# A hybrid attention and RWKV7 block: q and k stored once per pair and loaded by heads, the first inverse step behind two other operations, and another order of four up products

## The chip, the cores and the metric

The kernel runs on one core of one Trainium2 chip. TensorE (PE) multiplies, VectorE (DVE), ScalarE (ACT) and GpSimd (POOL) work on tiles, and SyncE (SP) issues most of the DMA transfers; POOL issues some of them too. Each engine takes its own instructions in order. The metric is the device time of one launch in microseconds (us). A profiled execution shows what every engine and every DMA queue did.

## The reference

One block of width 1024 over a sequence of 1024: a norm and modulation, then two token mixers side by side on the same input, gated and summed, then a feed-forward part with a causal convolution of width 3.

```python
def token_mixer(u, w_in, ...):
    proj = u @ w_in
    p_fox, p_rwkv, p_gate = _split(proj, (FOX_COLS, RWKV_COLS, GATE_COLS))
    q, k, v, f = _split(p_fox, FOX_SPLITS)
    log_f = jax.nn.log_sigmoid((f + fox_b_f).astype(jnp.float32)).transpose(0, 2, 1)
    o_fox = fox_attention(to_heads(q), to_heads(k), to_heads(v), log_f)
    o_rwkv = rwkv7_time_mix(p_rwkv, ...)
    gate_fox, gate_rwkv = jnp.split(jax.nn.sigmoid(p_gate), N_BRANCHES, axis=-1)
    merged = gate_fox * (o_fox @ fox_w_out) + gate_rwkv * (o_rwkv @ rwkv_w_out)
    return merged @ w_o

def fox_attention(q, k, v, log_f):
    cum = jnp.cumsum(log_f, axis=-1)
    ...
        logits = jnp.einsum('bhqd,bhkd->bhqk', q[:, :, q0:q1], k[:, :, :q1]).astype(jnp.float32) * scale
        logits = logits + cum[:, :, q0:q1, None] - cum[:, :, None, :q1]
    ...

def rwkv7_time_mix(...):
    ...
    def step(state, inp):
        r_t, w_t, k_t, v_t, a_t, b_t = inp
        sa = jnp.einsum('bhvk,bhk->bhv', state, a_t)
        state = state * w_t[:, :, None, :] + sa[..., None] * b_t[:, :, None, :] + v_t[..., None] * k_t[:, :, None, :]
        y_t = jnp.einsum('bhvk,bhk->bhv', state, r_t)
        return state, y_t
    ...

def conv_ffn(u, w_up, conv_w, conv_b, w_down):
    a, b = jnp.split(u @ w_up, 2, axis=-1)
    a = lax.conv_general_dilated(a, conv_w[:, None, :], ..., feature_group_count=D_FF) + conv_b
    return (jax.nn.silu(a) * b) @ w_down
```

There are 8 attention heads and 8 RWKV heads of width 64, and the hidden width of the feed-forward part is 2816.

## The kernel before, in words

**Precision.** A 32-bit operand is split into a high and a low part, both in the reduced 32-bit form that PE multiplies fast. A product is three matmul groups: high by high, low by high, high by low. So a weight `in` becomes `hi_in` (a cast) and `lo_in` (a subtraction on DVE, L274), and a projection tile of 128x512 takes 3 x 8 matmuls (the input is `u_hi`, `u_lo`).

**Stages**, by the profile's time: the norm and modulation to 60 us; the input projections to 600, with the RWKV recurrence woven between them; a transition to 626, with the last gates and the first head loads; attention to 825, with the rest of the gate products (`rk_ps`) between its steps; the branch outputs to 910 and w_o to 1005; the up products to 1430; the down products to the end.

**What sets the order.** PE's order is the order in which the program is written out; a planner in the program (`Weave`) decides by added-up matmul costs when the next piece of the recurrence is put between projection tiles. In the projections, the instructions of DVE, ACT, POOL and SP are put in order by the framework's scheduler, which takes the dependences between tiles and its own estimates; DVE and ACT in attention, and all engines in the up part, are written by hand. A wait is for a tile: a tile name has a fixed number of buffers, and the next user of a buffer waits until the last reader of the old content is done, be it an engine or a DMA that stores it.

**q and k** (`qk_steps`, L385 ff.; i from 0 to 3 for q, 4 to 7 for k; one i is a pair of heads, two halves of the sequence each). ACT writes the high part `qh` from PSUM (L393), DVE the low part `ql` (L395), and SP stores both (L399) into `d_st`, a DRAM array of [8 heads, 4 blocks, 128 rows, 1024]: blocks 0 and 1 hold, in 64-row halves, q high over q low and k high over k high; blocks 2 and 3 hold q high and k low, with 4 rows of forget-gate sums below each (L664, L665). So one half is six stores of 64x512. `qh` and `ql` share the tile name `sp0`. PSUM banks for projections (`big`) are two.

**A unit of the recurrence** is a pair of heads and a half of the sequence: 8 units. `pre` (L697 ff.) loads the decay `cum` and `al` from `d_lora` (L711, L713), scans `cum` (L715), takes exponentials (`el`, `en` L721), builds `ar` and `bk`, makes E from the products p (L764), and sends its 32x32 blocks through DRAM (`sm`, L772, and `M`, L776) to invert unit triangular matrices: 31 steps of a product t (L784) and a sum into E (L786) on DVE, one after the other. The result goes back through DRAM (`se`) into TT. Then come transposes of v and ar (`vt`, `at`), the products `q` and their copy into QA (L823), and the head sums `bs`, from which `bon` is made (L827). `main` (L829 ff.) takes it up later: X (L842), `xi` on PE, `zi`, the state S and its products `sp` (L903).

**Gates.** In the projections a gate tile `gt` goes through ACT and DVE (L337 to L341) and is stored as `d_gate<-gs` (L342) from a tile that the next gate uses. From the transition on, gate products are made in one bank `rk_ps`, which ACT reads twice (`gs` L1162, `gm` L1163) before PE may write the next one.

**Heads.** `load_head` (L993 ff.) brings one head's q, k and v for attention with three POOL transfers: `stA` 128x2x1024 (1 MB), `stB` 68x2x1024 (544 KB) and `vh` (512 KB); each has two buffers. Attention multiplies from `stA` over 128 rows and from `stB` over 68.

**The up products** (`plan`, L1606; `up_product`, `up_evac`): the 22 x 128 columns of each half of the up weight are made in pairs by a seven-product scheme with operands `T1` to `T4` of the activations and sums of weights (S1, A22 and so on). An entry (i, k) of `plan` is one product k of pair i. An operand is cast by ACT (L1722 for T, L1481 for weights) and its low part subtracted on DVE (L1485), in the order in which the plan needs them.

## Time and profile before

| what | us |
|---|---|
| median of 3 runs | 1646.45 |
| lowest and highest | 1645.22, 1648.16 |
| the profiled execution's own time | 1648.91 |
| its span in the trace | 1647.1 |
| head loads: median from issue to landing of stA, stB, vh | 6.9, 13.9, 3.9 |
| a 128 KB store of qh or ql | 2.5 |
| a copy M<-sm | 2.7 |

The span is the time from the first to the last instruction in the trace; the run's time has 1.8 us more around it. A row of the timeline gives the start, the duration, the engine, the line, the operation with output<-inputs and, in brackets, how long the engine had been idle before and what ended that. Line 141 holds all matmuls, line 145 all transposes, so PE's rows are told apart by their tiles. SPq and POOLq rows are the issue of a transfer, not its flight. The granted clock is a share of TensorE's full clock.

### The profile page before, as it was taken

The page shows a single profiled execution, that of the slowest core. Times are in us where ns is not written, and L with a number is a line of the kernel's source. Part 1 is how long each engine was busy: PE and PEld are TensorE (multiplying, and loading weights), DVE is VectorE, ACT ScalarE, POOL GpSimd, SP SyncE. Part 2 cuts the span into 40 slices and gives each one's busy share as a digit, 9 for nine tenths or more (in the row PEclk, how much of TensorE's full clock was granted, in tenths as well). Part 3 has the DMA queues.
Part 4 walks back from the last instruction along what each step waited for, and adds up shares of the span by engine and source line. Part 5 has one row for each costly group of instructions (what it writes and reads, how often), then busy time and mean ns, then how long its engine had stood idle before and what let it go on. Part 6 is the DMA issues. An engine that isn't in the chain of part 4 may idle for free.

```text
span 1647.1 us, 25947 instructions
## 1 busy us (share of the span) xinstructions
PE 1607.8 (98%) x9694; PEld 1339.6 (81%) x9694; DVE 1222.6 (74%) x2373; ACT 820.9 (50%) x1537; POOL 130.8 (8%) x153
## 2 busy tenths in 40 slices
PE   7999999999999999999999999999999999999998
PEld 7777788798978788888888888788888888888886
DVE  5786787878876526888679447887777777886677
ACT  5563335445445646766623235644444444555455
POOL 0011101111111010221022000000000000000000
PEclk9999999999999999999999999999999999999999
DMA  8488645543332346433197420242232232675363
GB/s 339 138 326 242 178 123 143 134 123 94 107 115 85 97 126 157 129 117 106 56 353 270 168 81 26 84 134 97 96 119 98 96 109 96 225 254 160 122 211 109
DMA packets 121645, 240.59 MB, mean 146 GB/s; under 512 B 40048, under 2 KB 48880, under 8 KB 121520
## 3 DMA queue, kind: packets, MB, share of 16 engines
q1 hardware_dynamic: 113040, 220.58, 41.0%
q0 software_dynamic: 8480, 18.37, 4.2%
q8 instruction: 76, 1.25, 0.3%
q14 instruction: 49, 0.40, 0.1%
HBM read 173.35 MB, written 65.54 MB: 145 GB/s over the span
## 4 chain that ended last, share of the span: by engine, by line
PE 58%; DVE 5%; ACT 2%; DMA 2%; issue 1%; SPq 0%; ACTq 0%; DVEq 0%
PE X L141 13%; PE D L141 13%; PE Y L141 6%; PE wo L141 5%; PE br L141 4%; PE rk_ps L141 3%; PE W L141 3%; PE gt L141 3%; PE lg L141 2%; PE ov L141 2%; PE tp L145 2%; DMA d_gate<-gs 1%; DVE nm L1049 1%; DVE P L1059 1%; DVE tl L1089 0%
## 5 line engine op out<-in xcount | busy, mean ns | idle before, releaser
L141 PE MATMUL D<-op,op 128*128 128x512 f32 x924 | 209.8, 389 | 0.0
L141 PEld LDWEIGHTS D<-op,op 128*128 128x128 f32 x924 | 173.3, 188 | 36.3 <-DVE op L1261 0.3
L141 PE MATMUL X<-T_m,S 128*128 128x512 f32 x440 | 107.8, 390 | 1.6 <-ACT T_m L1722 1.1
L141 PEld LDWEIGHTS X<-T_m,S 128*128 128x128 f32 x440 | 82.4, 188 | 20.4 <-ACT T_m L1722 2.5
L1260 ACT CAST op<-g 128x512 fp32r<-128x512 f32 x77 | 47.8, 621 | 73.8 <-PE D L141 49.0
L1261 DVE TENSOR_TENSOR op<-g,op 128x512 fp32r<-128x512 f32 x77 | 53.0, 688 | 41.4 <-ACT op L1260 41.4
L1519 DVE SCALAR_TENSOR_TENSOR c<-ab,vec,c 128x512 f32<-128x512 f32 x88 | 65.9, 750 | 18.4 <-ACT c L1522 16.8
L784 DVE TENSOR_TENSOR t<-E,M 128x60 f32<-128x60 f32 (+24 forms) x248 | 55.6, 224 | 27.9 <-DMA M<-sm 21.8
L1485 DVE TENSOR_TENSOR A<-ur,A 128x512 fp32r<-128x512 f32 x64 | 44.0, 688 | 38.7 <-ACT A L1481 38.5
L1485 DVE TENSOR_TENSOR S<-ur,S 128x512 fp32r<-128x512 f32 x66 | 45.5, 691 | 35.2 <-ACT S L1481 35.1
L274 DVE TENSOR_TENSOR lo_in<-raw_in,hi_in 128x512 fp32r<-128x512 f32 x84 | 56.7, 712 | 17.6 <-PE gt L141 4.8
L1481 ACT CAST S<-ur 128x512 fp32r<-128x512 f32 x66 | 41.0, 622 | 55.8 <-DVE ur L1474 30.6
L141 PE MATMUL Y<-T_h,S 128*128 128x512 f32 x264 | 63.6, 390 | 0.4 <-ACT T_h L1740 0.4
L141 PE MATMUL Y<-T_h,A 128*128 128x512 f32 x264 | 63.7, 389 | 0.3 <-ACT T_h L1722 0.3
L1053 ACT ACTIVATE P<-lg,nm 128x896 f32<-128x896 f32 (+3 forms) x64 | 47.4, 743 | 30.7 <-DVE nm L1049 22.5
L1481 ACT CAST A<-ur 128x512 fp32r<-128x512 f32 x64 | 39.6, 622 | 43.1 <-PE X L141 31.3
L786 DVE TENSOR_TENSOR E<-E,t 128x60 f32<-128x60 f32 (+24 forms) x248 | 56.2, 227 | 6.4
L141 PE MATMUL W<-B_f,A 128*128 128x512 f32 x252 | 60.6, 389 | 0.0
L141 PE MATMUL X<-B_b,A 128*128 128x512 f32 x252 | 60.5, 389 | 0.0
L141 PEld LDWEIGHTS Y<-T_h,S 128*128 128x128 f32 x264 | 49.5, 188 | 11.1 <-ACT T_h L1740 0.8
L141 PEld LDWEIGHTS Y<-T_h,A 128*128 128x128 f32 x264 | 49.5, 188 | 10.9 <-ACT T_h L1722 0.7
L272 ACT CAST hi_in<-raw_in 128x1024 fp32r<-128x1024 f32 x42 | 43.8, 1048 | 26.3 <-PE ps_rkv L141 11.3
(483 smaller groups left out, 4134.4 us busy)
## 6 DMA issues: line engine op xcount, KB each, us to landing
raw_in<-in_w_in SPq DMA_DIRECT2D x50, 512.0 KB, 4.0
wm<-in_w_mod SPq DMA_DIRECT2D x48, 512.0 KB, 7.3
ur<-in_w_up SPq DMA_DIRECT2D x44, 512.0 KB, 3.8
g<-d_g SPq DMA_DIRECT2D x35, 512.0 KB, 4.0
d_g<-gs SPq DMA_DIRECT2D x44, 256.0 KB, 2.0
d_g<-c SPq DMA_DIRECT2D x33, 256.0 KB, 4.4
d_st<-qh SPq DMA_DIRECT2D x64, 128.0 KB, 2.5
stA<-d_st POOLq DMA_DIRECT2D x8, 1024.0 KB, 6.9
```

The costliest lines, as they stand in the source:

```text
L141: nc.tensor.matmul(o, lhsT, rhs, start=start, stop=stop, skip_group_check=more)
L145: nc.tensor.transpose(o, i, eye)
L272: nc.scalar.copy(hi, raw)
L274: nc.vector.tensor_tensor(lo[:, c : c + NH], raw[:, c : c + NH], f32(hi[:, c : c + NH]), op=ALU.subtract)
L784: tt(tv, E32[:, 0:J, s : s + 1].to_broadcast([128, J, W]), M32[:, s : s + 1, s + 1 : 32].to_broadcast([128, J, W]), op=ALU.mult)
L786: tt(E32[:, 0:J, s + 1 : 32], E32[:, 0:J, s + 1 : 32], tv, op=ALU.add)
L1053: nc.scalar.activation(e[:, 0:n], lg[:, 0:n], AF.Exp, bias=nm[:, 0:1], accum_out=nm[:, 1:2])
L1260: nc.scalar.copy(hi, src)
L1261: tt(lo, src, f32(hi), op=ALU.subtract)
L1481: nc.scalar.copy(hi, src)
L1485: tt(lo, src, f32(hi), op=ALU.subtract)
L1519: stt(c, ab[:, x + hf * NH : x + hf * NH + NH], V("conv_w", 22 * x + i), c, op0=ALU.mult, op1=ALU.add)
```

## The change

1. `d_st` is replaced by `d_qk` [4 pairs, 4 parts, 128 rows, 1024], with the parts q high, q low, k high, k low of both heads of a pair, and `d_f` for the forget-gate rows. One half of q or k is stored with two transfers of 128x512 (256 KB) in place of six of 64x512 (128 KB).
2. `load_head` picks a head's 64 rows out of `d_qk`: `stA` in two transfers of 64x2x1024, `stB` in one of 64x2x1024 and one of the 4 rows of `d_f`, and `vh` as before.
3. The first step of the first unit's inverse (the product t, L784) is ordered on DVE behind the copy QA<-q (L823) and behind `bon` (L827) of that unit.
4. In `plan` the products (1, 4) and (0, 5) change places, so that both products with T4 come ahead of both with T1.

```diff
--- before.py
+++ after.py
@@ -201,7 +201,8 @@
 
 
     d_gate = dr.tile([16, 128, S], F32, name="d_gate")
-    d_st = dr.tile([8, 4, 128, S], F32R, name="d_st")
+    d_qk = dr.tile([4, 4, 128, S], F32R, name="d_qk")
+    d_f = dr.tile([8, 2, 4, S], F32R, name="d_f")
     d_v = dr.tile([8, 128, 8, 128], F32R, name="d_v")
     d_orw = dr.tile([4, 128, S], F32, name="d_orw")
 
@@ -242,6 +243,12 @@
             nc.vector.tensor_tensor(dst[:, cs], ps, bb[:, cs], op=ALU.add)
 
     marks = {}
+    first_step = []
+
+    def after_this(i):
+        for x in first_step:
+            tc.add_manual_dep(x.ins, i.ins.name, NOSYNC)
+
     late_lo = deque()
 
     def lower(wait=0):
@@ -393,10 +400,8 @@
                 nc.scalar.activation(hi, ps, AF.Copy, scale=sc_)
                 lo = gsp.tile([128, NH], F32R, tag="sp0", name=f"ql{i}_{hf}")
                 stt(lo, ps, sc_, f32(hi), op0=ALU.mult, op1=ALU.subtract)
-                h0 = 2 * (i % 4)
-                for t, k, r0 in ((hi, 0, 0), (lo, 0, 64), (hi, 2, 0)) if i < 4 else ((hi, 1, 0), (hi, 1, 64), (lo, 3, 0)):
-                    for h in range(2):
-                        nc.sync.dma_start(f32(d_st[h0 + h, k, r0 : r0 + 64, cs]), f32(t[h * 64 : h * 64 + 64, :]))
+                for t, x in ((hi, 0), (lo, 1)) if i < 4 else ((hi, 2), (lo, 3)):
+                    nc.sync.dma_start(f32(d_qk[i % 4, x, :, cs]), f32(t))
 
         HS = (slice(0, 64), slice(64, 128))
 
@@ -661,8 +666,8 @@
                     nc.scalar.copy(r[:, 3, :], z)
                     nc.scalar.activation(r[:, 4, :], f32(r[:, 0, :]), AF.Copy, scale=-1.0)
                     nc.scalar.activation(r[:, 5, :], f32(r[:, 1, :]), AF.Copy, scale=-1.0)
-                    nc.sync.dma_start(f32(d_st[:, 2, 64:68, cs]), f32(r[:, 0:4, :]))
-                    nc.sync.dma_start(f32(d_st[:, 3, 64:68, cs]), f32(r[:, 2:6, :]))
+                    nc.sync.dma_start(f32(d_f[:, 0, :, cs]), f32(r[:, 0:4, :]))
+                    nc.sync.dma_start(f32(d_f[:, 1, :, cs]), f32(r[:, 2:6, :]))
 
             for p in range(4):
                 for i in (p, 4 + p):
@@ -781,8 +786,10 @@
             for s in range(31):
                 J, W = s // 4 + 1, 31 - s
                 tv = t32[:, 0 : J * W].rearrange("p (j w) -> p j w", w=W)
-                tt(tv, E32[:, 0:J, s : s + 1].to_broadcast([128, J, W]),
-                   M32[:, s : s + 1, s + 1 : 32].to_broadcast([128, J, W]), op=ALU.mult)
+                i = tt(tv, E32[:, 0:J, s : s + 1].to_broadcast([128, J, W]),
+                       M32[:, s : s + 1, s + 1 : 32].to_broadcast([128, J, W]), op=ALU.mult)
+                if k == 0 and s == 0:
+                    first_step.append(i)
                 tt(E32[:, 0:J, s + 1 : 32], E32[:, 0:J, s + 1 : 32], tv, op=ALU.add)
             se = scr.tile([2, NCU, 2, 32, 32], F32, tag="se", name=f"se{n}")
             for g in range(4):
@@ -820,11 +827,12 @@
             for c in range(NCU):
                 for h in range(2):
                     mm(q[HS[h], c * CH : c * CH + CH], E[HS[1 - h], c, h, 0, :], UV[HS[1 - h], c, h, :], start=True, stop=True)
-            nc.vector.tensor_copy(QA[:, :, 0, :], c3(q))
+            after_this(nc.vector.tensor_copy(QA[:, :, 0, :], c3(q)))
             bp = gen(f"bs{n}")
             yield from head_sums(bp, rkb, tmp("kr", dt=F32R), tmp("al", dt=F32R))
             bon = tmp("bon", bufs=2)
-            tt(bon, bp, vv, op=ALU.mult)
+            after_this(tt(bon, bp, vv, op=ALU.mult))
+            first_step.clear()
             units[p, hf] = dict(ready=ready, pcd=pcd, ar=ar, E=E, QA=QA, TT=TT, bon=bon, UV=UV)
 
         def main(k, p, hf):
@@ -991,10 +999,13 @@
     heads = {}
 
     def load_head(h):
+        rows = d_qk[h // 2, :, h % 2 * 64 : h % 2 * 64 + 64, :].rearrange("k r s -> r k s")
         A = at.tile([128, 2, S], F32R, tag="stA", name=f"stA{h}")
-        nc.gpsimd.dma_start(A, d_st[h, 0:2, :, :].rearrange("k r s -> r k s"))
+        nc.gpsimd.dma_start(A[0:64, :, :], rows[:, 0:3:2, :])
+        nc.gpsimd.dma_start(A[64:128, :, :], rows[:, 1:3, :])
         B = at.tile([128, 2, S], F32R, tag="stB", name=f"stB{h}")
-        nc.gpsimd.dma_start(B[0:68, :, :], d_st[h, 2:4, 0:68, :].rearrange("k r s -> r k s"))
+        nc.gpsimd.dma_start(B[0:64, :, :], rows[:, 0:4:3, :])
+        nc.gpsimd.dma_start(B[64:68, :, :], d_f[h].rearrange("k r s -> r k s"))
         vh = at.tile([128, 8, 128], F32R, tag="vh", name=f"vh{h}")
         i = nc.gpsimd.dma_start(vh, d_v[h])
         marks.setdefault("head", i)
@@ -1604,7 +1615,7 @@
         put(6, s1[:, NH:])
 
     plan = [(i, k) for ks in ((1, 2), (7,), (6,)) for i in range(2) for k in ks]
-    plan += [(0, 4), (0, 5), (1, 5), (1, 4), (0, 3), (1, 3)] + [(2, k) for k in (1, 7, 6, 2, 4, 5)]
+    plan += [(0, 4), (1, 4), (0, 5), (1, 5), (0, 3), (1, 3)] + [(2, k) for k in (1, 7, 6, 2, 4, 5)]
     for i in range(3, NFF):
         plan += [(i, 1), (i, 7), (i - 1, 3)] + [(i, k) for k in ((6, 2, 4, 5) if i < NFF - 1 else (6, 2, 5, 4))]
     plan.append((NFF - 1, 3))
```

**DVE, the first unit's inverse** (t and E are its steps; `ql_0`, `ql_1` low parts of q/k halves, `lo_in` a weight's low part). Before:

```order
L395 SCALAR_TENSOR_TENSOR ql_0_1605<-qk_0_1461,qh_0_1603 128x512
L784 TENSOR_TENSOR t_0_1504<-E_0_1502,M_0_1497 128x31
L786 TENSOR_TENSOR E_0_1502<-E_0_1502,t_0_1504 128x31
L823 COPY QA_0_1426<-q_0_1638 128x8x64
...
L784 TENSOR_TENSOR t_0_1504<-E_0_1502,M_0_1497 128x48
L827 TENSOR_TENSOR bon_0_1679<-bs_0_1656,v_639 128x512
L786 TENSOR_TENSOR E_0_1502<-E_0_1502,t_0_1504 128x2x24
L274 TENSOR_TENSOR lo_in_1716<-raw_in_1713,hi_in_1715 128x512
L784 TENSOR_TENSOR t_0_1504<-E_0_1502,M_0_1497 128x69
L274 TENSOR_TENSOR lo_in_1716<-raw_in_1713,hi_in_1715 128x512
L395 SCALAR_TENSOR_TENSOR ql_1_1705<-qk_1_1613,qh_1_1703 128x512
```

After (the line numbers are those of the changed kernel):

```order
L402 SCALAR_TENSOR_TENSOR ql_0_1582<-qk_0_1438,qh_0_1580 128x512
L830 COPY QA_0_1407<-q_0_1611 128x8x64
L834 TENSOR_TENSOR bon_0_1652<-bs_0_1629,v_640 128x512
L789 TENSOR_TENSOR t_0_1481<-E_0_1479,M_0_1474 128x31
L281 TENSOR_TENSOR lo_in_1685<-raw_in_1682,hi_in_1684 128x512
L793 TENSOR_TENSOR E_0_1479<-E_0_1479,t_0_1481 128x31
L281 TENSOR_TENSOR lo_in_1685<-raw_in_1682,hi_in_1684 128x512
L402 SCALAR_TENSOR_TENSOR ql_1_1678<-qk_1_1586,qh_1_1676 128x512
L789 TENSOR_TENSOR t_0_1481<-E_0_1479,M_0_1474 128x30
```

QA stood behind the first step of the inverse, bon behind the product of the eighth, and ql_1 behind the product of the ninth; now QA and bon stand ahead of all steps, and ql_1 behind the first. Some 35 rows further on, the scan of the fourth unit's `cum`, which stood behind the product 128x48 (six blocks of width 8), stands behind the sum 128x4x19.

**SP, the stores of q and k around the first unit's blocks** (`sm`, `M`; `raw_in` a weight's load). Before:

```order
L399 DMA d_st<-qh_0_1394 64x512 x2
L399 DMA d_st<-ql_0_1396 64x512 x2
L399 DMA d_st<-qh_0_1394 64x512 x2
L711 DMA cum_0_2119<-d_lora 128x512
L399 DMA d_st<-qh_1_1444 64x512 x4
L399 DMA d_st<-ql_1_1446 64x512 x2
L772 DMA sm_0_1492<-E_0_1425 32x8x32 x4
L260 DMA raw_in_1814<-in_w_in 128x1024
L776 DMA M_0_1497<-sm_0_1492 32x1024 x4
```

After:

```order
L404 DMA d_qk<-qh_0_1379 128x512
L404 DMA d_qk<-ql_0_1381 128x512
L716 DMA cum_0_2080<-d_lora 128x512
L404 DMA d_qk<-qh_1_1425 128x512
L267 DMA raw_in_1775<-in_w_in 128x1024
L404 DMA d_qk<-ql_1_1427 128x512
L777 DMA sm_0_1469<-E_0_1406 32x8x32 x4
L781 DMA M_0_1474<-sm_0_1469 32x1024 x4
```

Twelve stores have become four, and the weight's load has moved from between `sm` and `M` to ahead of both.

**POOL, the first head's loads at the transition.** Before:

```order
L995 DMA stA_6836<-d_st 128x2x1024
L997 DMA stB_6838<-d_st 68x2x1024
L999 DMA vh_6840<-d_v 128x1024
L266 CAST hi_in_6895<-raw_in_6893 128x1024
L995 DMA stA_6966<-d_st 128x2x1024
```

After:

```order
L1004 DMA stA_6773<-d_qk 64x2x1024
L1005 DMA stA_6773<-d_qk 64x2x1024
L1007 DMA stB_6776<-d_qk 64x2x1024
L1008 DMA stB_6776<-d_f 4x2x1024
L1010 DMA vh_6779<-d_v 128x1024
L273 CAST hi_in_6834<-raw_in_6832 128x1024
```

Two more issues stand on POOL ahead of `vh` and of the cast behind it, for each head.

## Prediction

> **What bounds the kernel now.** I read the busy line of the page first, then the span in stages, then what TensorE (PE) waited for, and last the timeline around each of its long waits.
>
> ```profile
> PE 1607.8 (98%) x9694; PEld 1339.6 (81%) x9694; DVE 1222.6 (74%) x2373; ACT 820.9 (50%) x1537; POOL 130.8 (8%) x153
> ```
>
> PE is busy for 98% of the span of 1647.1 us. The change takes no matmul away, so only PE's idle time and the time in which it runs at a low clock can be won. The stages have, in this order: start and end, busy time of PE, weight load, DVE, ACT and POOL, the granted clock, the DMA share and GB/s.
>
> ```profile
> 180.00:240.00 60.00, 57.70 (x403) 46.11 (x403) 49.89 (x163) 22.79 (x38) 5.19 (x10) 0.97 0.62 162
> ...
> 600.00:626.00 26.00, 24.07 (x101) 19.43 (x100) 9.17 (x13) 13.74 (x24) 7.15 (x9) 0.94 0.89 207
> 626.00:825.00 199.00, 191.98 (x1188) 166.93 (x1187) 161.81 (x328) 134.26 (x307) 33.43 (x38) 1.00 0.38 109
> ```
>
> The first two have idle time and a clock below 1; attention, the third, has idle time at the full clock. The waits of PE (total, times, longest) name one instruction in each (rk_ps, qk and, in attention, ov):
>
> ```profile
> PE rk_ps L141 <- ACT gm L1163: 3.1, 3, 1.9
> ...
> PE qk L141 <- DVE ql L395: 2.3, 1, 2.3
> PE ov L141 <- DVE o L1122: 2.0, 1, 2.0
> ```
>
> **Term 1, the q/k evacuation at 189.** The timeline of that place (start, duration, engine, line, operation; in brackets the idle time before and what ended it):
>
> ```profile
> 179.66 0.39 PE L141 MATMUL bs<-al,blk_r 128*128 128x512 f32 x1
> 182.54 0.19 DVE L784 TENSOR_TENSOR t<-E,M 128x31 f32<-128x31 f32 x1 [6.66 <-DMA M<-sm]
> 182.88 0.68 DVE L823 COPY QA<-q 128x512 f32<-128x512 f32 x1
> 186.43 0.68 DVE L827 TENSOR_TENSOR bon<-bs,v 128x512 f32<-128x512 f32 x1
> 188.49 0.68 DVE L395 SCALAR_TENSOR_TENSOR ql<-qk,qh 128x512 fp32r<-128x512 f32 x1
> 189.22 3.61 PE L141 MATMUL qk<-u_hi,hi_in 128*128 128x512 f32 x8 [2.31 <-DVE ql L395]
> ```
>
> and three short windows, the second and third for term 4:
>
> ```profile
> 189.20:192.60 3.40, 3.38 (x8) 2.65 (x9) 2.99 (x14) 0.60 (x1) 0.00 (x0) 0.54 0.61 133
> 620.40:622.40 2.00, 0.07 (x2) 0.01 (x1) 0.30 (x1) 1.67 (x4) 0.00 (x0) 1.00 1.31 293
> 622.40:625.80 3.40, 3.40 (x9) 2.75 (x10) 1.90 (x3) 1.72 (x3) 0.00 (x0) 0.58 1.32 197
> ```
>
> DVE takes its instructions in order. The first inverse step of the first unit stands 6.66 us for the M copies. QA, bon and ql are queued behind it, and the next q/k product needs the bank that ql reads: PE stands 2.31 us. Then the clock is granted at 0.54, and the 8 matmuls, which take 1.98 us at the full clock (the row at 618.48 below), take 3.61. The price is 2.31 + 3.61 - 1.98 = 3.9 us, and about 0.3 for the ninth matmul, which the low clock still covers in part: 4.2.
>
> After the change QA and bon go first. The products of q stand ahead of those of bon on PE, and bon's bank is ready when the second bs matmul ends at 179.66 + 0.39 = 180.05. bon then ends at about 180.05 + 0.68 = 180.7, and the inverse step is next. Between it and ql stand one step and two lower parts, 0.3 + 2 x 0.7 us. Even if M still lands at 182.54, ql ends near 182.54 + 0.3 + 1.4 + 0.7 = 184.9, and PE wants the bank at 189.22 - 2.31 = 186.9. Two us of cover remain. **Term 1 is -4.2 us**; its bounds are 0 (something else holds the bank) and -4.2. The stores are the smaller half of it: they were 96 transfers of 64 rows on SP's queue and become 32 of 128 rows. As DMA issue costs only SP time, and SP is not what PE waits for, fewer issues alone are priced at nothing; what hides them is that SP issues ahead. They do let M land earlier, which I count only as margin.
>
> [...]
>
> **Term 2, a decay scan ahead of E, priced at 0.** In the new order on DVE the scan of the third unit's cum stands ahead of the E products of the first unit.
>
> ```profile
> 163.11 0.63 ACT L721 ACTIVATE en<-cum 128x512 f32<-128x512 f32 x1 [1.45 <-DVE bk L744]
> ...
> 164.32 1.29 DVE L764 TENSOR_TENSOR E<-p,cst 128x512 f32<-128x512 f32 x2 [0.59 <-PE p L141]
> ...
> 165.96 0.53 SPq L711 DMA_DIRECT2D cum<-d_lora  x1
> ...
> 168.92 1.28 DVE L715 TENSOR_TENSOR_SCAN cum<-cst,cum 128x256 f32<-128x256 f32 x2 [3.31 <-DMA cum<-d_lora]
> ...
> 170.70 0.27 PE L145 MATMUL vt<-cst,v 128*128 128x128 f32 x1
> ```
>
> Its load can go when ACT has read the old cum for en, at 163.74, and takes 2.96 us (165.96 to 168.92). So scan and E are done at about 166.7 + 1.28 + 1.29 = 169.3, and PE's transposes want the bank at 170.7: slack 1.4. If it landed as late as before, E would be done at 171.5 and PE would stand about 0.8 to 1.0 us. Bounds 0 to +1.0; taken 0, since SP's queue is shorter here by the removed stores.
>
> **Term 3, the first unit's inverse, priced at 0 with thin cover.** The inverse is a chain of 62 small DVE operations, and other DVE work is dropped into it. In the new order the fourth unit's cum scan comes into its first part, before the steps that it followed.
>
> ```profile
> 215.11 0.50 DVE L786 TENSOR_TENSOR E<-E,t 128x8 f32<-128x8 f32 x1
> ...
> 222.94 0.43 DVE L842 STREAM_TRANSPOSE X<-TT 32x256 f32<-32x256 f32 x1 [0.89 <-DMA TT<-se]
> ...
> 226.99 0.69 PE L141 MATMUL xi<-X,E 32*32 32x32 f32 x32
> ```
>
> and one row of DVE's waits (total, times, longest):
>
> ```profile
> DVE cum L715 <- DMA cum<-d_lora: 11.2, 4, 4.7
> ```
>
> The chain ends at 215.61 and X 7.76 us later, 3.6 us before PE's xi. With the chain's start 1.8 us earlier (182.54 to 180.75) and its content 0.5 us shorter, it ends at 213.3 plus the wait w of that scan, X at 221.1 + w, and PE wants it at 226.99 - 4.2 = 222.8. So w up to 1.7 us is free. I estimate that its load is issued near 194, when the third unit's exponentials have read the buffer, and lands 2.96 us later at 197, while DVE comes to the scan at about 195.7: w = 1.3 us. Bounds: 0, and 4.7 us, the longest of the four such waits before. Past 1.7 us each us costs PE one, and from about 2 us of idle the clock adds 1.7. **Term 3 is 0, between 0 and 3.0 + 1.7 = 4.7 us.**
>
> **Term 4, the store at the transition.** Loading a head was three POOL transfers and becomes five: 64-row pieces and a 4-row one.
>
> ```profile
> 606.95 1.00 POOL L997 DMA_DIRECT2D stB<-d_st  x1
> ...
> 607.50 0.32 SPq L342 DMA_DIRECT2D d_gate<-gs  x1
> ...
> 618.05 0.60 ACT L337 ACTIVATE gs<-gt 128x512 f32<-128x512 f32 x1 [4.64 <-DMA d_gate<-gs]
> ...
> 618.48 1.98 PE L141 MATMUL rk_ps<-u_hi,lo_in 128*128 128x512 f32 x8
> ...
> 621.27 0.58 ACT L1162 ACTIVATE gs<-rk_ps 128x512 f32<-128x512 f32 x1
> 621.74 0.59 ACT L1163 ACTIVATE gm<-rk_ps 128x512 f32<-128x512 f32 x1
> ...
> 622.39 3.33 PE L141 MATMUL rk_ps<-u_hi,hi_in 128*128 128x512 f32 x8 [1.93 <-ACT gm L1163]
> ```
>
> the window of its flight, and the head loads among the DMA issues (count, size, median us to landing):
>
> ```profile
> 606.20:618.00 11.80, 11.80 (x53) 9.76 (x52) 3.83 (x5) 4.00 (x7) 5.57 (x8) 1.00 1.03 268
> ```
>
> ```profile
> stA<-d_st POOLq DMA_DIRECT2D x8, 1024.0 KB, 6.9
> stB<-d_st POOLq DMA_DIRECT2D x8, 544.0 KB, 13.9
> vh<-d_v POOLq DMA_DIRECT2D x8, 512.0 KB, 3.9
> ```
>
> PE stands 1.93 us for gm, because ACT came late to the earlier gate: it waited 4.64 us until a 256 KB store, issued at 607.50, had landed and freed its tile. The store is in flight together with the first head. There the 68-row piece is odd: 544 KB in 13.9 us (39 KB/us), where 1024 KB of 128 rows take 6.9 and 512 KB take 3.9 (148 and 131 KB/us). [...] In 64 rows the 512 KB should land like vh, in about 4 us. The bytes stay: 11.8 us x 268 GB/s = 3.2 MB were moved by 618, and at the 293 GB/s of the window from 620.4 they take 10.8 us, so the store can be some 1 us earlier, and more where its engines were the loaded ones: landing at 615.5 to 617. ACT needs it only 0.8 us sooner: its next product ends at 618.48 + 1.98 = 620.46, gs and gm follow each other by 0.47 us (621.27, 621.74) and PE starts 0.65 after gm, so PE cannot go on before about 620.46 + 0.47 + 0.65 = 621.6. It still stands some 1.1 us, less than the 2.0 us at ov, which left that stage's clock at 1.00. Gain: 622.39 - 621.6 = 0.8, and the low clock, 3.33 - 1.98 and 0.3 for the matmul behind = 1.7. **Term 4 is -2.5 us**, between 0 (bytes, not few engines, hold the store) and -2.5.
>
> [...]
>
> The later heads' loads cost two more POOL issues each, 1.4 to 2 us at the 0.70 and 1.00 us of the rows above and below:
>
> ```profile
> 645.69 0.70 POOL L995 DMA_DIRECT2D stA<-d_st  x1 [16.66 <-PE lg L141]
> ...
> 678.62 0.22 PE L141 MATMUL lg<-stA 128*128 128x128 f32 x1
> ```
>
> The third head is loaded from 645.69 and first read at 678.62; with 14 us for the longest piece that leaves some 17 us of cover, so they are priced at 0.
>
> **Term 5, the up products, 0.** T4's two products go side by side ahead of T1's.
>
> ```profile
> 1053.63 0.58 ACT L1559 COPY x<-X 128x512 f32<-128x512 f32 x1
> ...
> 1054.26 3.04 PE L141 MATMUL X<-T_m,S 128*128 128x512 f32 x12 [0.52 <-ACT x L1559]
> ```
>
> Up to here PE's wait for T1 casts is partly covered, about 0.4 us. But the next thing that PE waits for is ACT's copy at 1053.63, at the end of a chain of ACT and DVE work that does not wait for PE; what PE wins before, it waits there (0.52 us now). Gain 0; a loss only where PE came more than 0.7 us later; bounds -0.4 and +0.5.
>
> **The sum** is -4.2 + 0 + 0 - 2.5 + 0 = -6.7 us against the profiled span of 1647.1: 1640.4. The median of the runs shown is 1646.45, 0.65 under that span, so the forecast is 1646.45 - 6.7 = **1639.8 us**. 0.2% is 3.3 us, about what a measurement here can tell from no change: 1643.15 is the line.
>
> **The rivals.**
> 1. *Only the q/k stall goes* (the store is held by bytes, not by few engines): 1646.45 - 4.2 = 1642.2. [...] Against: 0.8 us is enough. Chance 0.25.
> 2. *The inverse gives the gain back*: w of 3.5 us at the cum scan stops PE for 1.8 us at xi, half of the time with the low clock, so 2 to 3.5 us of 4.2 are lost: 1641.8 to 1645.7 with and without term 4, middle 1643.8. For it: one mean wait of that kind was 11.2 / 4 = 2.8, and the cover is 1.7. Against: its load is issued without a queue of 64 small stores ahead of it. Chance 0.16.
> 3. *Slower*: the same wait at 4.7 us costs 3.0 + 1.7 = 4.7 us at xi, more than term 1 won, and the store stays: 1646.45 + 0.5 = 1646.9. It decides from w = 4.2 us on, and passes +0.2% from w = 7.5. For it: nothing but that load's landing sets w. Against: no such wait before was over 4.7. Chance 0.08.
> 4. *The low clock is not the gap's*: PE runs 3.4 us at half clock at both places whatever it waited, and only 2.31 + 0.8 = 3.1 us go: 1643.3. For it: the 2.0 us wait at ov leaves the clock at 1.00, the 1.93 us one here does not, so the length alone does not decide. Against: the low clock begins with the matmul after the gap both times. Chance 0.05.
>
> The forecast has 0.40, and 0.06 stay for an order that I did not see through.
>
> **How the numbers follow.** The unknown costs add -0.4 below the forecast and to the rivals above; the runs before spread from 1645.2 to 1648.2, so some 1.5 us come on each side. Its own range is 1638.2 to 1641.5. The range that holds 8 in 10 goes on to rivals 1 and 2: 1637.5 to 1645. Faster by over 0.2%: the forecast's 0.40, rival 1's but for its upper edge, 0.23, a third of rival 2, 0.05, and 0.02 of rival 4: 0.70. Slower: a third of rival 3 and most of the unseen: 0.08. The rest, 0.22, is no change.
>
> **What would show it.** Right: no wait of PE for ql near 185 and a clock of 1.00 from 180 to 240; PE's wait for gm near 615 to 618 at about 1.1 us with a clock of 1.00 behind it; stB in 4 to 7 us; the up part as before at the copy of x. Wrong: a wait at xi of the first unit (near 222) behind a long DMA wait of the cum scan; a d_gate store that still takes over 9 us; a new PE wait for E or for vt near 170.

## The result, and the profile after

| | before | changed |
|---|---|---|
| median of 20 runs, us | 1648.04 | 1652.09 |
| lowest and highest, us | 1645.22, 1652.04 | 1648.48, 1654.93 |
| span of the profiled execution, us | 1647.1 | 1650.3 |

The changed kernel is slower: the ratio is 1.0021, with a 95% interval of 1.0014 to 1.0029. The forecast was 1639.8 us with a range of 1637.5 to 1645.0, so both its sign and its range failed.

PE issues the same matmuls in both kernels, but for the order of a few in the up products, so the start of each can be set against its counterpart. Counted from the first matmul, the changed kernel's PE is ahead (-) or behind (+) by, in us:

| place (time before) | ahead or behind | what stands there |
|---|---|---|
| 163 to 187 | +0.1 | nothing new near the scan ahead of E |
| 192.6 | -4.0 | the stall for ql and its half clock are gone |
| 251.7 | -3.1 | PE waits for S |
| 297.4 | -1.1 | PE waits for S again |
| 300.5 | +1.6 | half clock behind it |
| 440.7 | +2.1 | a wait in the v products |
| 622.4 | +3.0 | the wait for gm |
| 1042.7 | +3.2 | waits beside the exchanged products (+2.2 at 1032) |
| 1054.3 | +3.1 | the copy of x |
| end | +3.0 | |

So the stall at 189 did go, and everything was paid back within 110 us. First the place of the win. The timeline of DVE in the changed kernel (L789, L793, L834 and L402 are its lines of t, E, bon and ql):

```profile
180.40 0.69 DVE L834 TENSOR_TENSOR bon<-bs,v 128x512 f32<-128x512 f32 x1 [3.09 <-PE bs L141]
181.67 0.19 DVE L789 TENSOR_TENSOR t<-E,M 128x31 f32<-128x31 f32 x1 [0.58 <-DMA M<-sm]
...
183.12 0.68 DVE L402 SCALAR_TENSOR_TENSOR ql<-qk,qh 128x512 fp32r<-128x512 f32 x1
...
215.42 0.18 DVE L793 TENSOR_TENSOR E<-E,t 128x8 f32<-128x8 f32 x1
...
223.01 0.44 DVE L850 STREAM_TRANSPOSE X<-TT 32x256 f32<-32x256 f32 x1 [0.71 <-DMA TT<-se]
...
270.47 0.19 DVE L789 TENSOR_TENSOR t<-E,M 128x31 f32<-128x31 f32 x1 [6.24 <-DMA M<-sm]
```

ql ends at 183.8, long before PE wants its bank. But the first inverse begins only 0.87 us earlier than before (182.54) and ends at 215.60, as before (215.61). The third unit's inverse begins at 270.47; in the kernel before it was

```profile
270.71 0.77 DVE L784 TENSOR_TENSOR t<-E,M 128x31 f32<-128x31 f32 x1 [3.62 <-DMA M<-sm]
```

0.24 us later, although PE delivered E's products nearly 3 us earlier. DVE just waits longer for M. On SP's queue the third unit's blocks go out and come back like this, before and after the change:

```profile
261.72 1.78 SPq L772 DMA_DIRECT2D sm<-E  x4
...
265.42 2.99 SPq L776 DMA_DIRECT2D M<-sm  x4
```

```profile
260.19 1.92 SPq L777 DMA_DIRECT2D sm<-E  x4
...
265.46 1.71 SPq L781 DMA_DIRECT2D M<-sm  x4
```

sm is stored 1.5 us earlier, and M is fetched at the same time: SP's waits for sm to land were 1.8 us in all before and are 3.3 now. Why sm took longer to land was not followed. What PE then meets is on ACT, near 297 (ACT and PE of the changed kernel):

```profile
292.16 0.63 ACT L724 ACTIVATE el<-cum 128x512 f32<-128x512 f32 x1 [6.16 <-DVE ar L746]
293.74 0.62 ACT L745 COPY bk<-bk 64x512 f32<-64x512 f32 x1 [0.94 <-DVE bk L744]
...
295.65 0.63 ACT L726 ACTIVATE en<-cum 128x512 f32<-128x512 f32 x1 [0.22 <-DVE bk L749]
296.19 0.29 ACT L911 ACTIVATE S<-sp,pcd 128x64 f32<-128x64 f32 x1
```

```profile
291.51 0.33 PE L141 MATMUL sp<-S,Mt 128*128 128x64 f32 x2
...
296.54 0.69 PE L141 MATMUL sp<-S,Mt 128*128 128x64 f32 x2 [3.25 <-ACT S L911]
```

The product that S needs is done at 291.84. S runs at 296.19, because el, bk and en stand ahead of it on ACT and each waits for DVE, which is busy with the third inverse. Moving them away takes that wait with them, as e5 and e9 show below. Before, the same row was

```profile
297.36 0.43 PE L141 MATMUL sp<-S,Mt 128*128 128x64 f32 x2 [1.38 <-ACT S L903]
```

The windows (columns as in the prediction) show the price, before and after:

```profile
240.00:310.00 70.00, 68.31 (x673) 56.04 (x670) 56.13 (x152) 32.56 (x63) 9.48 (x14) 1.00 0.50 134
```

```profile
180.00:240.00 60.00, 59.83 (x485) 48.57 (x484) 50.52 (x160) 23.41 (x40) 4.70 (x10) 1.00 0.47 140
240.00:310.00 70.00, 65.85 (x561) 53.13 (x561) 54.15 (x153) 31.03 (x60) 9.52 (x14) 0.95 0.38 109
```

From 180 to 240 PE is whole and at the full clock. From 240 to 310 it is 2.5 us less busy, and the clock is at 0.95, which is 3.5 us of clock lost. Last the transition, on SP, ACT and PE, and the DMA issues of the head loads:

```profile
610.07 6.24 SPq L349 DMA_DIRECT2D d_gate<-gs  x2
...
621.33 0.60 ACT L344 ACTIVATE gs<-gt 128x512 f32<-128x512 f32 x1 [5.37 <-DMA d_gate<-gs]
...
625.67 3.04 PE L141 MATMUL rk_ps<-u_hi,hi_in 128*128 128x512 f32 x8 [2.66 <-ACT gm L1174]
```

```profile
stA<-d_qk POOLq DMA_DIRECT2D x16, 512.0 KB, 6.7
...
stB<-d_qk POOLq DMA_DIRECT2D x8, 512.0 KB, 9.5
vh<-d_v POOLq DMA_DIRECT2D x8, 512.0 KB, 3.8
```

The store lands 11.2 us after its issue, not earlier than the 10.5 of before, and PE waits 2.66 us. A 512 KB piece of 64 rows takes 6.7 or 9.5 us, not the 3.8 of vh.

### The profile page after: what moved, and what is told of

It is laid out like the page before. It is cut to its first block, busy times and chain, and to the rows that moved or that the text cites. A ratio compares the mean times of both kernels' runs of the same rounds, so it can differ in the third digit from the quotient of the medians.

```text
span 1650.3 us, 25895 instructions
## 1 busy us (share of the span) xinstructions
PE 1608.9 (97%) x9694; PEld 1340.3 (81%) x9694; DVE 1220.0 (74%) x2373; ACT 820.6 (50%) x1537; POOL 137.0 (8%) x169
## 4 chain that ended last, share of the span: by engine, by line
PE 60%; DVE 5%; ACT 2%; DMA 1%; issue 1%; SPq 0%; ACTq 0%; DVEq 0%
PE X L141 13%; PE D L141 13%; PE Y L141 7%; PE wo L141 5%; PE br L141 5%; PE rk_ps L141 3%; PE W L141 3%; PE gt L141 3%; PE lg L141 2%; PE ov L141 2%; PE tp L145 2%; DMA d_gate<-gs 1%; DVE nm L1060 1%; DVE P L1070 1%; DVE tl L1100 0%
## 5 line engine op out<-in xcount | busy, mean ns | idle before, releaser
L789 DVE TENSOR_TENSOR t<-E,M 128x60 f32<-128x60 f32 (+24 forms) x248 | 54.9, 222 | 24.0 <-DMA M<-sm 17.9
L793 DVE TENSOR_TENSOR E<-E,t 128x60 f32<-128x60 f32 (+24 forms) x248 | 55.7, 225 | 6.4
```

The costliest lines, as they stand in the source:

```text
L789: i = tt(tv, E32[:, 0:J, s : s + 1].to_broadcast([128, J, W]), M32[:, s : s + 1, s + 1 : 32].to_broadcast([128, J, W]), op=ALU.mult)
L793: tt(E32[:, 0:J, s + 1 : 32], E32[:, 0:J, s + 1 : 32], tv, op=ALU.add)
```

## The experiments

Every run lists the span and the mean granted clock. From these each time is split in two: what the clock took, span x (1 - clock), and the rest, which stands for the time at the full clock. The split is rough, since a low clock also counts where it costs nothing: from 1640 to 1647 us, where PE issues no matmul, the clock is 0.75 in the profile before and 0.66 in that of e13_again. The clock has three digits (0.001 is 1.6 us of one run). The table gives the ratio to the kernel before on the same chip and, for each part, the difference of the means, in us; the standard errors of these differences are 0.4 to 0.7 us of the rest and 0.5 to 1.0 us of the clock's part. The ratio is not the quotient of these means: for e12 the two parts add up to +0.7 us where the ratio gives -0.3, so differences below 1 us are not read from either.

| run | what | ratio (95%) | clock's part | rest |
|---|---|---|---|---|
| e1_order | before + ordering of the first step | 1.0015 (1.0006, 1.0024) | +2.2 | +0.5 |
| e2_layout | before + new layout | 1.0015 (1.0006, 1.0023) | +0.3 | +2.0 |
| e3_plan | before + new plan | 1.0003 (0.9994, 1.0011) | -0.6 | +1.3 |
| e4_loads | before + five loads from d_st | 1.0021 (1.0013, 1.0030) | +1.0 | +2.8 |
| e5_states | changed + S ahead on ACT | 1.0011 (0.9998, 1.0024) | +1.7 | +0.2 |
| e9_states2 | changed + S ahead, gentler | 1.0007 (0.9994, 1.0019) | +1.1 | 0.0 |
| e10_split_b | before + stB cut | 1.0006 (0.9994, 1.0018) | +1.3 | -0.1 |
| e11_split_a | before + stA cut | 1.0030 (1.0019, 1.0041) | +2.9 | +2.1 |
| e12_gate2 | changed + gate tile elsewhere | 0.9998 (0.9987, 1.0010) | +0.9 | -0.2 |
| e14_before_gate2 | before + gate tile elsewhere | 0.9993 (0.9984, 1.0002) | +0.3 | -1.1 |
| e13_repaired | changed + e9 + e12, old plan | 1.0002 (0.9991, 1.0012) | +2.5 | -3.2 |
| e13_again | the same | 1.0001 (0.9990, 1.0013) | +2.8 | -2.7 |
| e16_layout_repaired | e13 without the ordering | 1.0003 (0.9994, 1.0011) | +0.1 | +0.2 |
| e15_no_order | before + e9 + e12 | 0.9999 (0.9990, 1.0009) | +1.1 | -0.9 |

The changed kernel's own 20 runs have 9.6 us of clock and 1640.6 of rest, where the kernel before has 6.9 to 7.6 and 1640.1 to 1640.8 in the sets beside the runs of the table. That would put most of its loss on the clock; but its own runs of the kernel before list no clock, so this is a comparison across sets and not shown.

### One part at a time

e1_order is the third part of the diff alone, e2_layout the first two, e3_plan the fourth. e4_loads cuts the loads but leaves the stores:

```diff
-        nc.gpsimd.dma_start(A, d_st[h, 0:2, :, :].rearrange("k r s -> r k s"))
+        nc.gpsimd.dma_start(A[0:64, :, :], d_st[h, 0:2, 0:64, :].rearrange("k r s -> r k s"))
+        nc.gpsimd.dma_start(A[64:128, :, :], d_st[h, 0:2, 64:128, :].rearrange("k r s -> r k s"))
...
-        nc.gpsimd.dma_start(B[0:68, :, :], d_st[h, 2:4, 0:68, :].rearrange("k r s -> r k s"))
+        nc.gpsimd.dma_start(B[0:64, :, :], d_st[h, 2:4, 0:64, :].rearrange("k r s -> r k s"))
+        nc.gpsimd.dma_start(B[64:68, :, :], d_st[h, 2:4, 64:68, :].rearrange("k r s -> r k s"))
```

> The kernel before with only the first inverse step ordered behind QA and bon. Theory A (the win at 189 is paid back by PE's waits for the state S near 250 and 297, since DVE's inverses of the second and third unit come hardly earlier): no wait for ql at 189 (PE 4 us ahead there), but the wait of sp for S near 297 grows from 1.4 to about 3 us and the clock is halved behind it; in all +0 to +2 us. Rival B (the loss is the new layout's, through its stores and loads): -4 us, with the S wait near 297 at most 1.5 us and the full clock there.

> The kernel before with only the new layout (two 128-row stores, five loads per head). Theory A: the stall at 189 stays or shrinks by under 2 us, the S wait near 297 stays at 1.4 us plus what PE won, and the transition's wait for gm grows from 1.9 to 2.7 us: 0 to +1.5 us in all. Rival B: +5 us or more, most of it behind the stores or in attention.

> The kernel before with only (1,4) and (0,5) exchanged in plan. From the difference of the two traces PE loses about 2 us between 1033 and 1039, wins 1.3 back at 1042, and ends 0.6 us later: +0.6 us. Rival (the forecast): what PE loses or wins before 1054 goes into its wait for ACT's copy there: 0 us.

> The kernel before with only the head loads cut into five (64, 64, 64, 4 rows and vh) out of the old array. Theory C (the gate's store is held by the bytes of the head loads on all engines): the store still lands 10 us or more after its issue, PE's wait for gm stays at 1.9 us or more, 0 to +1 us. Rival D (few engines hold it, as forecast): the store lands in under 9.5 us, the wait falls to 1.1 us and the clock stays full: -2.5 us.

None of the parts is a gain by itself. **The ordering** (e1) takes the stall at 189 away, and PE meets the first unit's X and then S, by PE's timeline:

```profile
225.12 0.22 PE L141 MATMUL xi<-X,E 32*32 32x32 f32 x2 [1.14 <-DVE X L851]
226.31 0.80 PE L141 MATMUL xi<-X,E 32*32 32x32 f32 x30 [0.97 <-DVE X L851]
...
300.10 0.44 PE L141 MATMUL sp<-S,Mt 128*128 128x64 f32 x2 [2.37 <-ACT S L912]
```

Its rest is the same within its error, and its clock's part is 2.2 us larger. What PE no longer waits for ql it waits elsewhere: its waits for X and S near here add up to 2.1 + 2.9 us, where the kernel before has 2.3 for ql and 1.7 for S. Theory A holds in the main: +2.5 us by the ratio (1.0 to 4.0), where it had 0 to +2. The wait at S near 300 was 2.4 us, not 3, with the full clock behind it; the low clock came behind xi, from 226.7 to 230.1. **The five loads** cost as much as the whole change: the store lands 11.9 us after its issue and PE waits 3.34 us. Theory D, the forecast's, falls; theory C has the late store right, but its 0 to +1 us was too little. **The layout** as a whole is between 1 and 4 us slower. What its stores take back of the loads' cost cannot be told from nothing; rival B's 5 us are out. **The plan** cannot be told from no change.

e3 and e4 have, up to 600 us, the program of the kernel before. They show the stall of 189 in two more executions (e3 first, then e4):

```profile
189.07 2.11 PE L141 MATMUL qk<-u_hi,hi_in 128*128 128x512 f32 x8 [2.01 <-DVE ql L395]
```

```profile
191.69 2.11 PE L141 MATMUL qk<-u_hi,hi_in 128*128 128x512 f32 x8 [2.14 <-DVE ql L395]
```

The same eight matmuls take 2.11 us behind a wait of 2.0 or 2.1 us: full clock. The 3.61 us of the profile before were one execution's.

### The S updates ahead on ACT

e5 and e9 are the changed kernel with ACT's work for later units ordered behind S updates; e9 leaves en where it does not delay the next load of cum:

```diff
+            i = nc.scalar.activation(el[:, :, 1:], c3(cum), AF.Exp, scale=-DEC)
+            if k == 4:
+                tc.add_manual_dep(i.ins, marks["S", 1, 0].ins.name, NOSYNC)
...
+            if k == 4:
+                tc.add_manual_dep(i.ins, marks["S", 1, 2].ins.name, NOSYNC)
...
+                if k == 1 and c == 1:
+                    tc.add_manual_dep(marks["bk", 3].ins, marks["S"].ins.name, NOSYNC)
```

> The changed kernel, with ACT's work for the units after next (el, en, the copy of bk, the cast kr) ordered behind the first S updates of units 1 and 2, so that S no longer waits on ACT for DVE. Theory A (PE's win at 189 is lost at the S wait near 297, 3.2 us and a half clock behind it): that wait falls under 1.5 us, the clock stays full there, and the time falls by 2.5 to 5 us against the changed kernel, to about 1648. Rival (DVE's late inverses stop PE at the next place anyway, xi or E of the next unit): the wait reappears within 30 us, under 1 us is won.

> The changed kernel with only the second unit's S updates ahead on ACT: el behind S0, the copy of bk behind S1, the cast kr and en behind S2, so that en, and with it the next load of cum, comes no later. If the S wait near 297 is only a matter of ACT's order: it falls from 3.2 to under 1 us, no wait of 2 us or more follows up to 320, and the time is 2 to 5 us under the changed kernel. If DVE is what is late (its inverse of the third unit starts only 0.2 us earlier than before the change): a wait of about the same size follows within 15 us, as the one of yp for S did, and under 1.5 us is won.

In e5 the longest wait of sp for S was 0.9 us, and one of 3.1 us came at yp, 13 us behind the old place; in e9 (PE's waits: total, times, longest)

```profile
PE yp L141 <- ACT S L917: 2.2, 1, 2.2
PE sp L141 <- ACT S L917: 2.2, 3, 1.0
```

Against the changed kernel's 1.0021 the ratios are 1.6 and 2.3 us lower, each with an uncertainty of about 2.5 us, so that a win is possible but not shown. The rivals hold for the wait, which goes on to the next thing that hangs on DVE; their limits for the time, 1 and 1.5 us, are not decided. In e5 one reason is seen, a scan of cum that waited for its load because en, the reader of the old cum, had been put back:

```profile
304.56 1.27 DVE L722 TENSOR_TENSOR_SCAN cum<-cst,cum 128x256 f32<-128x256 f32 x2 [2.86 <-DMA cum<-d_lora]
```

### The gate's store

e10 and e11 cut one of the two large head loads each. e12 and e14 give the last gate before the transition a tile of attention's memory (the output tile o, first used later); no order changes on any engine:

```diff
-            g = pool.tile([128, NH], F32, tag=tag, name=f"gs{i}_{hf}")
+            g = (at.tile([128, NH], F32, tag="o", name=f"gs{i}_{hf}") if (i, hf) == (8, 1) else
+                 pool.tile([128, NH], F32, tag=tag, name=f"gs{i}_{hf}"))
```

> The kernel before with only stB's load cut into 64 and 4 rows. [...]

> The kernel before with only stA's load cut into two of 64 rows. [...] Rival (the number of transfers counts): the store 1 to 1.5 us later, +1 to +2 us.

> The changed kernel with one tile elsewhere: the last gate before the transition (half 1 of gate 8) gets a tile of attention's memory that is free by then, and no order changes on any engine. Theory C (the five loads cost through the gate's store: ACT waits for it, PE waits for ACT): ACT's wait before that gate falls from 5.4 to under 2 us, PE's wait for gm from 2.7 to 1.1 us, and the time by 1 to 3 us. Rival (the loads cost elsewhere, or the wait goes to the tile's next user): under 0.5 us.

> The kernel before with only that tile elsewhere. Theory C: its wait for gm, 1.2 to 1.9 us, comes down to 1.1 us: 0 to -1.5 us, less than the changed kernel wins by it. If the tile itself wins, whatever the loads: as much as there.

ACT's wait for the store in e10 and in e11:

```profile
620.65 0.60 ACT L337 ACTIVATE gs<-gt 128x512 f32<-128x512 f32 x1 [5.67 <-DMA d_gate<-gs]
```

```profile
621.90 0.60 ACT L337 ACTIVATE gs<-gt 128x512 f32<-128x512 f32 x1 [8.40 <-DMA d_gate<-gs]
```

The stores had been issued at 609.09 and 607.61, so they took 11.5 and 14.2 us; PE waited 2.96 and 5.69 us for gm. With three loads the store took 8.5 us in e1 and 8.1 in e3, and PE waited 1.18 us in both. The author held before them that stB's 68 rows decide: its cut alone should bring the store to 10.5 us or more, and a cut of stA alone should leave it at 8 to 9. That was an estimate; e10 fits it in the store and the wait, and e11 does not: cutting stA, which leaves the 68-row piece as it was, delays the store more (14.2 us) than cutting stB does (11.5). Why a cut load holds up a store on another queue is not settled by these runs.

That the loads cost by way of the store is. In e12 ACT no longer waits for it, and PE goes on as soon as its own product allows:

```profile
615.53 0.60 ACT L345 ACTIVATE gs<-gt 128x512 f32<-128x512 f32 x1 [1.64 <-PE gt L141]
...
622.11 2.11 PE L141 MATMUL rk_ps<-u_hi,hi_in 128*128 128x512 f32 x8 [1.18 <-ACT gm L1175]
```

With that tile alone the changed kernel is level with the kernel before (0.9998), which by the same tile wins at most a little (0.9993, with 1 inside the interval). Theory C as e12 states it, that the five loads cost through the gate's store, holds. The wait at S near 296 was still 3.1 us in e12.

A first try of this had gone wrong. e6_gate, e7_both and e8_before_fixed (the last two with e5's ordering too) gave the tile to the gate before. Its place in memory was probably still in use by the last unit; the profile names no such wait, but ACT started right behind that unit's last product gg on DVE (614.19 to 614.89). ACT began that gate at 615.09, and PE waited 3.5 us (in e6) for the gate's DVE step, which began at 617.75. The ratios were 1.0036 (1.0024, 1.0048), 1.0043 (1.0026, 1.0059) and 1.0036 (1.0023, 1.0050), a cost of the wrong tile that says nothing on the theories.

> The changed kernel, with the first gate tile behind the head loads in a buffer of its own, so that ACT does not wait for the store that the head loads delay. Theory C (the five loads delay the store, and that costs PE at 620): the wait for gm falls from 2.7 to 1.2 us or less, and the time falls by 1.5 to 3 us. Rival (the loads cost elsewhere, in attention): under 0.7 us.

> The changed kernel with both of the repairs and the old order of the up products. If theories A and C hold and are independent: 4 to 7 us under the changed kernel, that is 1645 to 1648, and under the kernel before. If the waits only move: 1650 to 1652.

> The kernel before with the same two repairs and nothing of the change. Theory A and C: its S waits (0.8 and 1.4 us) and its wait for gm (1.2 to 1.9 us) shrink: -1.5 to -3.5 us against before. It is the measure for what the change itself is worth once its two debts are paid: e7 should be 1 to 3 us faster than this one if the ordering and the stores are a gain, equal or slower if not.

### Both repairs, with and without the ordering

e13 is the changed kernel with e9's and e12's repairs and the old plan. e16 takes the ordering out of it (nothing is put into first_step), and e15 has the repairs on the kernel before.

> The changed kernel with that tile, the S updates of the second unit ahead on ACT (as in the run before that) and the old order of the up products. If both debts are paid: 1647 to 1649, at or under the kernel before by up to 2 us. If PE's lead is lost to DVE in any case: no better than the one with the tile alone.

> The repaired changed kernel once more, as the measure for the next two on the same chip: again within 2 us of the kernel before.

> The repaired changed kernel without the ordering of the first inverse step (new layout, both repairs, old plan). If the ordering is a gain once the S wait is repaired: 1 to 3 us slower than the repaired kernel, with the stall for ql back at 1.4 us. If PE's lead is lost to DVE before the second unit ends in any case: equal within 1 us, or faster.

> The kernel before with both repairs and nothing of the change. If the new layout's stores are a gain: 1 to 2 us slower than the one with the layout. If not: equal. Against the kernel before: 0 to -2 us, by the S waits (0.8 and 1.4 us).

The three are level with each other and with the kernel before. But they get there in different ways. With the ordering the rest is 2.7 to 3.2 us under the kernel before, and the clock takes 2.5 to 2.8 us more; without it neither moves by more than twice its error. PE's waits from 180 to 330 in e13_again and then in e16:

```profile
PE yp L141 <- ACT S L918: 3.1, 1, 3.1
PE sp L141 <- ACT S L918: 0.9, 1, 0.9
```

```profile
PE qk L141 <- DVE ql L403: 2.0, 1, 2.0
PE qk L141 <- DVE v L377: 1.5, 1, 1.5
PE sp L141 <- ACT S L916: 1.1, 1, 1.1
PE q L141 <- ACT UV L822: 0.7, 1, 0.7
```

So by this split the ordering takes about 3 us out of the rest once its debts are paid, and it does not show in the time. A part of this can be the split's own: in the profiles of e13_repaired and e13_again the last 5.4 and 5.3 us, without a matmul, stood at half clock, where the kernel before had 3.6 and e16 3.9. Half of that length is counted, so 0.7 to 0.9 us of the extra clock there cost no time. The long wait that the ordering leaves at yp was followed by the low clock in e13_repaired (2.0 us) and not in e13_again (3.1 us); the last section has what the records show of such waits. Where the extra low clock of e13 falls in most executions is left open. No version here beats the kernel before by more than the measurement can tell.

## Why the prediction was wrong

- **Term 1** was right in its mechanism: no wait for ql, the clock at 1.00 from 180 to 240, PE 4.0 us ahead at 192.6 (4.2 predicted). It was mis-sized as a property of the kernel: e3 and e4 pay 2.0 and 2.1 us there at the full clock. The step that failed is "Then the clock is granted at 0.54", taken from one execution and counted whole. The inverse began when M had landed, at 181.67, and not right behind bon as the sum had it (180.75).
- **Term 2** held: no wait of PE for E or vt near 170.
- **Term 3** is where the win went, by a way it did not follow. Its wait w for the scan was 0.1 us, not 1.3. But the chain was not "0.5 us shorter": it took 215.60 - 181.67 = 33.9 us against 33.1. In it DVE was busy for 31.8 us against 31.5 and idle for 2.1 against 1.5, of which 0.4 us was a wait for a q/k product of PE; QA and bon had left it, but QA of the next unit came in (212.14). xi waited 0.2 us. The step that failed is the end of the sum at the first unit's xi. That PE's lead would last was never worked out for the units behind it, whose inverses start when M lands: 0.24 us earlier in the third unit, against a PE that was 3 us ahead. Rival 2 named the right debtor, the inverse, but with a wrong place and price. The "from about 2 us of idle the clock adds 1.7" of this term was an estimate, taken from the two waits of the profile before; behind 2.37 us in e1 and 2.48 in e2 the clock stayed at 1.00.
- **Term 4** had the wrong sign. The steps that failed are "In 64 rows the 512 KB should land like vh, in about 4 us" (9.5 us) and from it the store at 615.5 to 617, 8.0 to 9.5 us after its issue. It landed 11.2 us after its issue, and 11.0 and 11.9 in e2 and e4. That few engines held the store was the author's estimate, and no run shows which engines a transfer is on; the runs show that beside cut loads the store took 10.7 us or more, and beside whole ones 10.5 or less. The reference was off too: the profile before had the store at 10.5 us, where e1 and e3 with the same loads had 8.5 and 8.1. What the chain would be without the store was right: 1.1 us predicted, 1.18 measured in e12.
- **Term 5** had the right place for PE's waits on casts, but not the new one for Ze_a: PE's waits from 1030 to 1054 sum to 0.28 + 0.90 + 0.18 + 0.52 = 1.88 us before and to 0.30 + 0.39 + 0.58 + 1.16 + 0.18 = 2.61 after. That is +0.7 us in the trace, and e3's ratio cannot tell it from nothing.
- **Rival 4** deserved more: at both places the low clock was not the gap's alone. Gaps of 2.0 and 2.1 us at 189 left the clock full in e3 and e4, and the table of the last section sets it beside where a gap fell in time. The low clock began at 189.45 and 622.95, after the matmul behind the gap had started (189.22 and 622.39), and not with it. Rival 1's price was right only in that the store did not come earlier.
- **The range** was built as if the costs were unknown only between the rows of one execution. The parts may not be additive either: e1 and e2 together would be some 5 us, while the change is 3.5 (1652.09 / 1.0021 against it), but the intervals are too wide to show it. A reason for it would be that the inverse begins 1.4 us earlier than in e1 with the new stores (181.67 against 183.09) and that xi waits 0.2 us in place of 2.1.

## What to carry to other kernels

A stall that is removed on the busiest engine is won only if the engine that it waited for also gets ahead: follow the freed time to the next two or three hand-overs, with the arrival of each, before it is counted. A clock that was low behind a wait in one execution (0.54 at 189 here, and 1.00 in e3 and e4) is a chance, not a cost: look at a second trace of the same program before it is counted whole, and split each run's time into what the clock took and the rest, without the stretches in which PE has nothing to do. Where a transfer is re-cut, look for stores that are in flight beside it and for who waits to reuse their tiles; another buffer there was worth as much here as the transfer's form (1.0021 without it, 0.9998 with it in e12).

## What the runs showed of the hardware

**Of PE's waits of 1.9 us and more some were followed by the low clock and some were not, whatever their length; in the clock's records the low stretches begin on a grid of 3.41 us.** Waits of PE and what followed, over the profiles named: 1.93 us (before, 622) low; 2.01 and 2.14 (e3, e4, 189) full; 2.31 (before, 189) low; 2.37 (e1, 300) full; 2.48 (e2, 625) full; 2.66 and 3.25 (changed, 625 and 297) low; 2.0 (e13_repaired, yp) low; 3.1 (e13_again, yp) full; 3.34 (e4, 627) low. The length alone does not sort them.

In the profile before, the stretches at 0.50 begin at 42.68, 189.45, 622.95 and 1643.53 us, which are 43, 127 and 299 times 3.413 us apart; in the profile after they begin at 42.91, 295.50, 626.59 and 1647.17, which are 74, 97 and 299 times that apart. Those that end within the span last 3.41 or 6.83 us. Cut on that grid, the stretches between 60 and 1640 us with 1.3 us or more without a matmul are these:

| profile | stretch, us | without a matmul, us | the wait in it | clock of the next stretch |
|---|---|---|---|---|
| before | 186.04 to 189.45 | 2.30 | 2.31, ql | 0.50 |
| before | 619.53 to 622.95 | 1.93 | 1.93, gm | 0.50 |
| before | 674.15 to 677.56 | 1.74 | 1.98, ov | 1.00 |
| before | 295.27 to 298.68 | 1.38 | 1.38, S | 1.00 |
| after | 623.18 to 626.59 | 2.49 | 2.66, gm | 0.50 |
| after | 292.08 to 295.50 | 2.21 | 3.25, S | 0.50 |
| after | 677.79 to 681.20 | 1.35 | 1.97, ov | 1.00 |

Two things stand beside this. After 295.50 the low clock went on through a second stretch, with 1.04 us without a matmul in the first; and in e15 it began at 327.8, where PE was idle for 1.2 us in all from 320 to 330. Neither is explained.

Four more waits can be laid on the grids of their own profiles, read to 0.1 us from windows of 5 us. Those of e1, e2 and e3 that the full clock followed are cut by a border, at 298.4, 624.0 and 187.6 us, and have at most 1.7, 1.5 and 1.5 us on one side of it; the 2.0 us at yp in e13_repaired lie whole ahead of a border at 306.0, and the low clock begins there.

The wait at ov near 676 takes 1.97 or 1.98 us in each of the ten profiles with such windows. The low clock followed it in six (e1, e3, e12, e13_repaired, e13_again, e15) and not in the other four (before, changed, e2, e16). With a limit of 1.8 us, between the 1.74 and the 1.93 of the table, and with a grid that can lie anywhere, a wait of 2.0 us would draw the low clock in about half of the executions (an estimate from these figures: (3.41 + 2.0 - 2 x 1.8) / 3.41 = 0.53).

**The cut transfers gained little here, and a store beside them took longer.** stA's 1 MB took 6.9 us whole (before) and its two halves 6.7 us each (changed; medians of all heads); stB took 13.9 us with 68 rows and 9.5 with 64, while vh, the same 512 KB, took 3.8. A 256 KB store beside them took 8.1 to 10.5 us with the loads whole (before, e1, e3) and 10.7 to 14.2 with them cut (changed, e2, e4, e5, e9, e10, e11). The two ranges all but touch, so one profile of each would not have shown it.
